# Spreading the stores of turned outputs over several steps, and one more step inside the block inverse, in a hybrid mLSTM / gated DeltaNet layer on one Trainium2 core

## The chip, the cores and the metric

The kernel runs on one core of a Trainium2 chip. The core has a matrix engine (TensorE, PE in the profile), a vector engine (VectorE, DVE), a scalar engine (ScalarE, ACT), a general one (GpSimd, POOL) and a synchronization engine (SyncE, SP) that here does nothing but issue transfers. ACT issues transfers too, from the same queue from which it computes. The metric is the device time of one execution in microseconds; lower is better. A time is given as the median of several runs.

## The reference

One layer on x of 512 tokens by 2048, all in float32. The input is normalised and multiplied by one combined weight matrix `w_in`; the parts of the product feed two mixers of tokens. The mLSTM has 8 heads (query and key 128 wide, value 256), the gated DeltaNet 16 heads of 128. Their gated, normalised outputs are multiplied by the two halves of `w_out`, merged with gates, added to x and normalised. What matters here is the DeltaNet's solve with a unit lower triangular matrix in each chunk:

```python
kk = jnp.einsum('cbhtd,cbhsd->cbhts', kc, kc)
a_mat = jnp.where(strict, bc[..., :, None] * kk * decay_mat, 0.0)
lhs = a_mat + jnp.eye(CHUNK, dtype=a_mat.dtype)
sol = lax.linalg.triangular_solve(lhs, rhs, left_side=True, lower=True, unit_diagonal=True)
...
y_a = jnp.matmul(h_a, w_out[:ML_WIDTH])
y_b = jnp.matmul(h_b, w_out[ML_WIDTH:])
return jax.nn.sigmoid(gate_a) * y_a + jax.nn.sigmoid(gate_b) * y_b
```

## The kernel before

The large projections make three matmuls for each weight tile: weights and inputs are each split into a high and a low part (`uh`, `ul` for the input; `wh` for a weight, cast by ACT in L135; `wl`, the remainder, by DVE in L138), and high by high, low by high and high by low are added up in PSUM (L261 to L263). The first half of the program makes the projections that need no mixing. Then come eight units of mixing, about 1060 to 1960 us; the output projection is the rest.

A unit projects K, V and Q of two DeltaNet heads, and in most units the query and key of one mLSTM head (`proj_cm`, called again and again). Behind every six matmuls of a projection stands a call of `tick()`: that is what is called a step here. Small pieces of mixing work are Python generators that `start` puts on a list; a tick resumes each one that is due, and `yield n` says in how many steps it wants to be resumed. So the order of PE's instructions is written by hand, as the generators yield. The order of the other engines is made by a scheduler from priorities and dependences: `urgent` raises a priority, and `behind("A")` places an instruction behind the newest cast of a weight on ACT (L135).

`dn_back` makes the inverse of the triangular matrix of a chunk by blocks, for both heads of the unit at once. Its first product p1 is negated by ACT (s1), its second p2 is copied by ACT and DVE into `tb` and `ta` (L955, L951), its third p3 (L959) is negated by ACT into s3 (L962), and its fourth p4 (L966) reads s3 and is copied into `tb` (L968). Two steps later `dn_chain` starts for the first head and three steps later for the second: the recurrence over the four chunks (matmuls L990 to L1009, ACT's copy w L1001).

`ml_head` mixes one mLSTM head. Its values v are loaded by L1107 into the one buffer `v1`. At its end two halves of the output, 128 columns each, are multiplied by their gates (L1155) and given to `turn`.

`turn` transposes blocks of 32x32 on DVE into a buffer `to` (L796; there are two) and starts `travel`, which finishes the transposition through DRAM: four transfers of 64 KB (L806), one for each 32 partitions. For K and Q these go out on SP, to `td`, and are read back (L811). For a turned output (`out` is true) they go out on ACT, behind the newest cast, to `hm_d` for the mLSTM and `h_d` for the DeltaNet, 3 or 5 steps after the transposition.

Transfers of SP and ACT share eight counters in turn (in the program's order they are called DMAHW0 to DMAHW7). An instruction that issues a transfer waits in its engine's queue until the one before on its counter has landed, where nothing else has told it so already; what is behind it on that engine waits as well.

Other names in the prediction: `yp` (L770) is ACT's copy of a finished projection out of PSUM, which frees the PSUM buffer for PE; `wr` is a weight tile on its way in (L174); `gb`, `nrb`, `iwb` are loads of one row for all partitions; `gz` (L1016) is a load of a DeltaNet head's gate.

Of the kernel before, what the change touches and what calls it, by code (L numbers as in the profile page):

```python
# [17 lines left out]
NC = S // P  # L18
# [24 lines left out]
BS = 32  # L43
# [12 lines left out]
def hybrid_body(  # L56
# [16 lines left out]
    nc = tc.nc  # L73
    ctx.enter_context(tc.manual_schedule(engines={mybir.EngineType.PE}))
    V, A, G, T = nc.vector, nc.scalar, nc.gpsimd, nc.tensor
# [64 lines left out]
    def behind(eng):  # L140

        return tc.issue_after(newest[eng])
# [66 lines left out]
    def urgent(level=1):  # L209
        return tc.high_priority(offset=level * PRIO)  # L210
# [6 lines left out]
    def start(gen, wait=0, by=None):  # L217
        active.append([gen, clock["t"] + wait, held["by"] if by is None else by])
# [557 lines left out]
    def silu_end(dst, then=None):  # L776
        th = wkb.tile([P, S], F32, tag="th", name="th", bufs=2)
        with behind("A"):
            A.activation(th, dst, AF.Tanh)
        V.scalar_tensor_tensor(out=dst, in0=th, scalar=1.0, in1=dst, op0=ALU.add, op1=ALU.mult)  # L780
        if then is not None:
            turn(*then)
        yield 1
# [8 lines left out]
    def turn(src, dst, out=False, lag=5):  # L792


        o = dst if dst is not src and len(dst.shape) == 3 else wk.tile([P, NC, P], F32, tag="to", name="to", bufs=2)
        V.transpose(o if len(src.shape) == 3 else o.rearrange("p n c -> p (n c)"), src)  # L796
        start(travel(o, dst, out), lag if out else 2)

    def travel(o, dst, out):

        d = dst if len(dst.shape) == 4 else dr.tile([16, BS, 4, BS], F32, tag="td", name="td", bufs=8)
        ov = o.rearrange("p n (j c) -> p (n j) c", c=BS)
        q = nc.scalar if out else nc.sync
        with behind("A") if out else urgent(2):
            for a in range(4):
                q.dma_start(d[:, :, a, :].rearrange("m r c -> r m c"), ov[a * BS:(a + 1) * BS])  # L806
        if d is dst:
            return
        yield 4
        with behind("A") if out else urgent(2):  # L810
            q.dma_start(dst, d.rearrange("(n j) r a c -> (j r) n (a c)", n=NC))  # L811
        yield 1

    def dn_front_k(hs, kq, u):
# [108 lines left out]
    def dn_back(hs, kq, u):  # L923
# [36 lines left out]
        s3 = wk.tile([P, 2 * NC, 64], F32, tag="s3", name="s3", bufs=1)  # L960
        with urgent():
            A.mul(s3[64:128], p3[64:128], -1.0)  # L962
        yield 2
        p4 = psw.tile([P, 2 * NC, 64], F32, tag="wk", name="p4")
        for g, a in G2:
            T.matmul(p4[0:64, g, :], s3[64:128, g, :], tb[64:128, g, 64:128], start=True, stop=True)  # L966
# [9 lines left out]
    def dn_chain(j, hs, kq, u):  # L976
# [54 lines left out]
        with urgent():  # L1031
            V.tensor_tensor(out=g, in0=po, in1=g, op=ALU.mult)
        turn(g, h_d[h], True, 5 if h < 2 * UNITS[-1][0] else 3)

    def dn_unit(p, mh):
# [13 lines left out]
        if mh is not None:  # L1049
            ps = proj_cm(mh, kind="m")  # L1050
            mkq = wkb.tile([P, 2, S], F32, tag="mkq", name="mkq", bufs=1)
            with urgent():
                A.mul(mkq[:, 1, :], ps[0], float(P) ** -0.5)
            with urgent():
                A.copy(mkq[:, 0, :], ps[1])
            start(ml_head(mh, mkq), 1, "B")
# [10 lines left out]
        for j in range(2):  # L1067
# [3 lines left out]
            start(silu_end(kq[j][:, 1, :], (kq[j][:, 1, :], qn)), 4 + 3 * j, front)  # L1071
        start(dn_front_q(hs, kq, u), QWAIT + 3 * last, by)
        start(dn_back(hs, kq, u), (25 if mh is None else 9) + 4 * last, by)

    def ml_head(h, kq):
        kT, qT = kq[:, 0, :], kq[:, 1, :]
        kw = wkb.tile([P, NC, P], F32, tag="mkw", name="kw", bufs=1)
        with behind("V"):
            turn(kT, kw)
# [73 lines left out]
        for i in range(2):  # L1153
            with behind("V"):
                V.tensor_tensor(out=g[i], in0=v1[:, :, i * P:(i + 1) * P], in1=g[i], op=ALU.mult)  # L1155
            turn(g[i], hm_d[2 * h + i], True)
            yield 1

    def ml_first(h):

        kq = wkb.tile([P, 2, S], F32, tag="mkq", name="mkq", bufs=1)
        for i in range(2):
            nc.sync.dma_start(kq[:, 1 - i, :], qk_d[2 * QKFIRST * i + h])
        yield 4
        yield from ml_head(h, kq)
# [481 lines left out]
```

## Time and profile before

| | |
|---|---|
| median of 3 runs | 2236.08 us (2230.81 to 2239.41) |
| the profiled execution | 2233.9 us |
| its span (first to last instruction) | 2232.1 us |
| PE busy | 2159.3 us, 97% of the span |
| DVE busy | 1671.0 us, 75% |
| ACT busy | 995.0 us, 45% |
| POOL busy | 276.6 us, 12% |
| mean transfer rate | 195 GB/s |

Rows of the timeline give the start, the duration, the engine (with a q: its queue of transfers), the line, the operation, output and inputs, how many were grouped, and in brackets how long the engine stood idle before, and what ended that. Rows of waits give who waited for whom, the time in total, how often, and the longest. Rows of windows give a stretch, its length, the busy time (and number of instructions) of PE, PEld (the loading of weights into PE), DVE, ACT and POOL, then the granted clock of PE, the DMA share and GB/s. Where an engine that waits isn't PE, the time costs nothing by itself.

### The profile page before, as it was taken

The numbers are of one execution on the slowest core, as the hardware profiler recorded it, in microseconds if no ns is written. First come the engines' busy times: TensorE is split into PE (matmuls) and PEld (weight loads), VectorE is DVE, ScalarE is ACT, GpSimd is POOL, SyncE is SP. The second block draws the span as 40 slices with busy tenths as digits, with TensorE's granted clock in tenths as the row PEclk, the third lists the DMA queues.
The fourth block names the chain that finished last, engine by engine and source line by source line (L and its number), as shares of the span: only waits on it lengthen the run. The fifth ranks groups of instructions, "written<-read, shape, count | busy, mean of one in ns | idle before, by whom it ended". The sixth has DMA issues, their size and how long they took to land. (4 is left out here: it accounts for less than half of the span.)

```text
span 2232.1 us, 31548 instructions
## 1 busy us (share of the span) xinstructions
PE 2159.3 (97%) x10592; PEld 1771.9 (79%) x10592; DVE 1671.0 (75%) x2907; ACT 995.0 (45%) x1890; POOL 276.6 (12%) x356
## 2 busy tenths in 40 slices
PE   7999999999999999999999999999999999999997
PEld 5877878888788788788878887878888887877775
DVE  5787788888878777877588876757675868667875
ACT  5444444444444343444544544444444445344344
POOL 0320000000000000000222422222222211110101
PEclk9999999999999999999999999999999999999999
DMA  5456666667667766776776767676756568695896
GB/s 156 125 174 193 199 201 201 205 202 231 197 208 228 235 210 205 229 244 192 195 189 168 179 145 174 147 172 166 178 139 167 141 153 230 186 278 184 250 317 215
DMA packets 534821, 435.81 MB, mean 195 GB/s; under 512 B 241921, under 2 KB 393698, under 8 KB 534530
## 3 DMA queue, kind: packets, MB, share of 16 engines
q1 hardware_dynamic: 425058, 357.68, 56.4%
q10 hardware_dynamic: 105568, 68.77, 9.8%
q0 software_dynamic: 4032, 7.34, 2.2%
q8 instruction: 83, 1.36, 0.3%
q14 instruction: 80, 0.66, 0.1%
HBM read 342.37 MB, written 95.49 MB: 196 GB/s over the span
## 5 line engine op out<-in xcount | busy, mean ns | idle before, releaser
L135 ACT CAST wh<-wr 128x512 fp32r<-128x512 f32 (+1 forms) x538 | 379.9, 707 | 470.9 <-PE pj L262 261.8
L138 DVE TENSOR_TENSOR wl<-wr,wh 128x512 fp32r<-128x512 f32 (+1 forms) x538 | 447.2, 834 | 178.2 <-ACT wh L135 160.2
L261 PE MATMUL pj<-uh,wh 128*128 128x512 f32 x1024 | 431.6, 421 | 4.2 <-ACT yp L770 4.2
L263 PE MATMUL pj<-uh,wl 128*128 128x512 f32 x1024 | 404.3, 395 | 0.0
L262 PE MATMUL pj<-ul,wh 128*128 128x512 f32 x1024 | 403.2, 394 | 0.0
L576 PE MATMUL ps<-wl,uh 128*128 128x512 f32 x704 | 277.3, 394 | 7.2 <-DVE wl L138 7.0
L575 PE MATMUL ps<-wh,uh 128*128 128x512 f32 x704 | 276.3, 392 | 7.0 <-DVE X L617 6.5
L577 PE MATMUL ps<-wh,ul 128*128 128x512 f32 x704 | 275.0, 391 | 0.0
L135 ACT CAST wh<-ts 128x512 fp32r<-128x512 f32 x224 | 138.2, 617 | 256.3 <-DVE ts L535 192.2
L135 ACT CAST wh<-t 128x1024 fp32r<-128x1024 f32 x112 | 117.9, 1053 | 250.9 <-PE ps L577 122.8
L263 PEld LDWEIGHTS pj<-uh,wl 128*128 128x128 f32 x1024 | 194.1, 190 | 43.3
L261 PEld LDWEIGHTS pj<-uh,wh 128*128 128x128 f32 x1024 | 195.2, 191 | 40.8 <-ACT yp L770 5.4
L576 PE MATMUL ps<-wl,suh 128*128 128x512 f32 x576 | 224.2, 389 | 1.6 <-DVE wl L138 1.6
L575 PE MATMUL ps<-wh,suh 128*128 128x512 f32 x576 | 224.5, 390 | 0.8 <-ACT qk L353 0.3
L577 PE MATMUL ps<-wh,sul 128*128 128x512 f32 x576 | 224.1, 389 | 0.0
L262 PEld LDWEIGHTS pj<-ul,wh 128*128 128x128 f32 x1024 | 195.6, 191 | 33.4
L138 DVE TENSOR_TENSOR wl<-ts,wh 128x512 fp32r<-128x512 f32 x224 | 153.6, 689 | 38.0 <-ACT wh L135 38.0
L138 DVE TENSOR_TENSOR wl<-t,wh 128x1024 fp32r<-128x1024 f32 x112 | 137.6, 1229 | 48.0 <-ACT wh L135 47.4
L576 PEld LDWEIGHTS ps<-wl,uh 128*128 128x128 f32 x704 | 132.6, 188 | 43.1 <-DVE wl L138 16.7
L575 PEld LDWEIGHTS ps<-wh,uh 128*128 128x128 f32 x704 | 132.5, 188 | 40.5 <-DVE X L617 12.7
L577 PEld LDWEIGHTS ps<-wh,ul 128*128 128x128 f32 x704 | 132.5, 188 | 26.7
L535 DVE TENSOR_TENSOR ts<-wr 128x512 f32<-128x512 f32 x112 | 77.2, 690 | 99.8 <-DMA wr<-t_d 76.0
(302 smaller groups left out, 3462.5 us busy)
## 6 DMA issues: line engine op xcount, KB each, us to landing
wr<-in_w_in_dram SPq DMA_DIRECT2D x704, 256.0 KB, 3.7
wr<-in_w_out_dram SPq DMA_DIRECT2D x138, 256.0 KB, 4.8
t_d<-ts ACTq DMA_DIRECT2D x96, 256.0 KB, 4.4
wr<-t_d SPq DMA_DIRECT2D x96, 256.0 KB, 4.1
wr<-in_w_in_dram SPq DMA_DIRECT2D x64, 128.0 KB, 3.2
xt<-in_x_dram SPq DMA_DIRECT2D x8, 512.0 KB, 7.2
tg_d<-X ACTq DMA_DIRECT2D x16, 256.0 KB, 6.1
tg_d<-to ACTq DMA_DIRECT2D x16, 256.0 KB, 5.1
```

The lines of the kernel that those rows point to most:

```text
L135: newest["A"] = A.copy(hi, src).ins
L138: newest["V"] = V.tensor_tensor(out=lo, in0=src, in1=hi.bitcast(F32), op=ALU.subtract).ins
L261: T.matmul(ps[j], hi[:, k, wsl], uh[:, kt, :], start=(kt == 0), stop=False)
L262: T.matmul(ps[j], hi[:, k, wsl], ul[:, kt, :], start=False, stop=False)
L263: T.matmul(ps[j], lo[:, k, wsl], uh[:, kt, :], start=False, stop=(kt == KT - 1))
L535: V.tensor_tensor(out=ts[:, 0, :], in0=r[:, 0, :], in1=r[:, 2, :], op=ALU.subtract)
L575: T.matmul(ps[t], ah, hi, start=(g == "A" and i == 0), stop=False, skip_group_check=True)
L576: T.matmul(ps[t], ah, lo, start=False, stop=False, skip_group_check=True)
L577: T.matmul(ps[t], al, hi, start=False, stop=(i == KH - 1), skip_group_check=True)
```

## The change

Three edits. In `travel`, a turned output's four transfers are no longer issued at one tick: each is issued by itself, behind the cast that is newest then, and the next follows one step later. The last unit's heads, with a lag of 3 steps, still issue all four at once. In `ml_head` the second half of the output is multiplied and turned four steps after the first and not one. In `dn_back` the fourth product comes three steps after the third and not two. The transfers of K and Q are written a second time and do what they did. No instruction is added or removed. Line numbers behind `travel` grow by four, so that s3 becomes L966 and the fourth product L970.

```diff
-        start(travel(o, dst, out), lag if out else 2)
-
-    def travel(o, dst, out):
+        start(travel(o, dst, out, lag > 3), lag if out else 2)
+
+    def travel(o, dst, out, apart):
 
         d = dst if len(dst.shape) == 4 else dr.tile([16, BS, 4, BS], F32, tag="td", name="td", bufs=8)
         ov = o.rearrange("p n (j c) -> p (n j) c", c=BS)
-        q = nc.scalar if out else nc.sync
-        with behind("A") if out else urgent(2):
+        if out:
             for a in range(4):
-                q.dma_start(d[:, :, a, :].rearrange("m r c -> r m c"), ov[a * BS:(a + 1) * BS])
-        if d is dst:
+                with behind("A"):
+                    nc.scalar.dma_start(d[:, :, a, :].rearrange("m r c -> r m c"), ov[a * BS:(a + 1) * BS])
+                if apart:
+                    yield 1
             return
+        with urgent(2):
+            for a in range(4):
+                nc.sync.dma_start(d[:, :, a, :].rearrange("m r c -> r m c"), ov[a * BS:(a + 1) * BS])
         yield 4
-        with behind("A") if out else urgent(2):
-            q.dma_start(dst, d.rearrange("(n j) r a c -> (j r) n (a c)", n=NC))
+        with urgent(2):
+            nc.sync.dma_start(dst, d.rearrange("(n j) r a c -> (j r) n (a c)", n=NC))
         yield 1
...
         with urgent():
             A.mul(s3[64:128], p3[64:128], -1.0)
-        yield 2
+        yield 3
         p4 = psw.tile([P, 2 * NC, 64], F32, tag="wk", name="p4")
...
             turn(g[i], hm_d[2 * h + i], True)
-            yield 1
+            yield 4
```

How this moves instructions is seen in the program's order. On ACT around s3 of unit 4, before (`hm_d<-to` is one piece of a turned output, with the counter or engine that it waits for in brackets; `wh<-wr` is the cast of a weight):

```order
L806 DMA hm_d_68<-to_14633 32x16x32 [waits DMAHW6_49,DVE_49]
L806 DMA hm_d_68<-to_14633 32x16x32 [waits DMAHW0_49]
L806 DMA hm_d_68<-to_14633 32x16x32 [waits DMAHW2_49]
L806 DMA hm_d_68<-to_14633 32x16x32 [waits DMAHW4_49]
L955 COPY tb_9101<-p2_14727 32x8x32 [waits DVE_49]
L955 COPY tb_9101<-p2_14727 32x8x32
L135 CAST wh_14768<-wr_14714 128x512 [waits DMAHW5_49,PE_49,Activation_49]
L806 DMA hm_d_68<-to_14647 32x16x32 [waits DMAHW7_49]
L806 DMA hm_d_68<-to_14647 32x16x32 [waits DMAHW2_49]
L806 DMA hm_d_68<-to_14647 32x16x32 [waits DMAHW4_49]
L135 CAST wh_14803<-wr_14765 128x512 [waits DMAHW3_49,PE_49,Activation_49]
L806 DMA hm_d_68<-to_14647 32x16x32 [waits DMAHW6_49]
```

and s3 follows. With the change:

```order
L806 DMA hm_d_68<-to_14633 32x16x32 [waits DMAHW6_49,DVE_49]
L959 COPY tb_9101<-p2_14727 32x8x32 [waits DVE_49]
L959 COPY tb_9101<-p2_14727 32x8x32
L135 CAST wh_14765<-wr_14711 128x512 [waits DMAHW5_49,PE_49,Activation_49]
L806 DMA hm_d_68<-to_14633 32x16x32 [waits DMAHW6_49]
L806 DMA hm_d_68<-to_14633 32x16x32 [waits DMAHW7_49]
L135 CAST wh_14798<-wr_14762 128x512 [waits DMAHW3_49,DMAHW4_49,PE_49,Activation_49]
L806 DMA hm_d_68<-to_14633 32x16x32 [waits DMAHW3_49]
L806 DMA hm_d_68<-to_14725 32x16x32 [waits DMAHW4_49]
L966 ACTIVATE s3_14792<-p3_14783 64x512 [waits PE_49,Activation_49]
```

Five pieces stand ahead of s3 where eight stood, and three of the second half's four come behind it. The last one ahead of it waits for counter 4.

On SP, the loads of the same place, before, with v ahead of the list:

```order
L1107 DMA v1_15434<-v_d_70 128x4x256 [waits DVE_49]
L1016 DMA gz_15068<-gz_d_72 128x4x128 [waits DVE_49]
L806 DMA td_14695<-qn_14540 32x16x32 [waits DVE_49]
L806 DMA td_14695<-qn_14540 32x16x32
L806 DMA td_14695<-qn_14540 32x16x32 [waits DMAHW3_49]
L806 DMA td_14695<-qn_14540 32x16x32 [waits DMAHW4_49]
L174 DMA wr_14800<-in_w_in_dram 128x2x128 [waits DMAHW5_49,DVE_49]
L174 DMA wr_14800<-in_w_in_dram 128x2x128 [waits DMAHW7_49]
L760 DMA gb_14861<-rows_d_66 128x512 [waits DMAHW1_49,Pool_49]
L174 DMA wr_14846<-in_w_in_dram 128x2x128 [waits DMAHW3_49,DVE_49]
L811 DMA qn_14540<-td_14695 128x4x128 [waits DMAHW5_49,DMAHW4_49,DMAHW2_49]
L174 DMA wr_14846<-in_w_in_dram 128x2x128 [waits DMAHW6_49]
```

and with the change, from the weight load on:

```order
L174 DMA wr_14795<-in_w_in_dram 128x2x128 [waits DMAHW4_49,DVE_49]
L174 DMA wr_14795<-in_w_in_dram 128x2x128 [waits DMAHW5_49]
L760 DMA gb_14859<-rows_d_66 128x512 [waits DMAHW7_49,Pool_49]
L815 DMA qn_14540<-td_14692 128x4x128 [waits DMAHW2_49,DMAHW3_49,DMAHW1_49,DMAHW0_49]
L174 DMA wr_14831<-in_w_in_dram 128x2x128 [waits DVE_49]
L174 DMA wr_14831<-in_w_in_dram 128x2x128
L760 DMA nrb_15205<-rows_d_66 128x512 [waits Pool_49]
L1111 DMA v1_15434<-v_d_70 128x4x256 [waits DMAHW4_49,DVE_49]
```

The load of v, which waits for DVE's second product of the mLSTM head, has moved behind both weight loads; it is on counter 4, on which ACT's last piece ahead of s3 then waits.

On ACT at the first mLSTM output, around the copy yp at 1138 us, before:

```order
L135 CAST wh<-wr 128x512 x4
L806 DMA hm_d<-to 32x16x32 x3
L770 COPY yp_9097<-pj 128x512
L806 DMA hm_d<-to 32x16x32
L135 CAST wh<-wr 128x512
```

and with the change:

```order
L135 CAST wh<-wr 128x512 x4
L806 DMA hm_d<-to 32x16x32
L770 COPY yp_9097<-pj 128x512
L771 ACTIVATE kq_9106<-yp_9097,convc 128x512
L135 CAST wh<-wr 128x512
L806 DMA hm_d<-to 32x16x32
```

One piece stands ahead of the copy where three stood.

On PE, two times six matmuls of a projection stood between the third product and the fourth, and now three times six; the fourth product and all that starts behind it in a unit come six matmuls later. Everything else on PE that the change does not name keeps its place.

## The prediction

> **What bounds the kernel now.** First comes the page's first part: TensorE (PE) is busy for nearly the whole span, so only the time in which it stands, or runs below its full clock, can be won.
>
> ```profile
> PE 2159.3 (97%) x10592; PEld 1771.9 (79%) x10592; DVE 1671.0 (75%) x2907; ACT 995.0 (45%) x1890; POOL 276.6 (12%) x356
> ```
>
> The change touches only the stage in which the heads are mixed, from about 1060 to 1960 us. The view of waits, cut to that window and to PE, tells what PE stood for there (us in total, times, longest):
>
> ```profile
> PE p L966 <- ACT s L962: 7.8, 4, 2.6
> PE pj L261 <- ACT yp L770: 4.2, 3, 2.1
> PE pr L990 <- DVE st L1009: 2.4, 1, 2.4
> PE py L1306 <- ACT yp L770: 2.3, 2, 1.7
> PE pw L998 <- DVE tb L968: 1.4, 1, 1.4
> ```
>
> The sum of these five rows is 18.1 us, 0.8% of the span. The largest is the very pair that the change spreads: the fourth product of the block inverse (L966) waits for ACT's negation s3 (L962) of the third product. The timeline of PE has the four places, in units 3 to 6 of the eight; the number in brackets is how long PE stood:
>
> ```profile
> 1466.07 1.14 PE L966 MATMUL p<-tb,s 64*64 64x64 f32 x16 [2.59 <-ACT s L962]
> ...
> 1578.01 1.14 PE L966 MATMUL p<-tb,s 64*64 64x64 f32 x16 [1.67 <-ACT s L962]
> ...
> 1687.88 1.14 PE L966 MATMUL p<-tb,s 64*64 64x64 f32 x16 [1.25 <-ACT s L962]
> ...
> 1800.39 1.14 PE L966 MATMUL p<-tb,s 64*64 64x64 f32 x16 [2.25 <-ACT s L962]
> ```
>
> A stop costs more than its own length where PE's clock falls behind it. The windows view of the 3.4 us behind five of these stops and one other shows it (the row at 1139.9 follows the 2.07 us wait for yp, 1389.1 the 2.4 us wait of L990, the rest follow the four rows above; the last three columns are granted clock, DMA share and GB/s):
>
> ```profile
> 1139.90:1143.30 3.40, 3.40 (x10) 2.62 (x9) 2.92 (x7) 3.26 (x7) 0.00 (x0) 0.51 1.08 164
> 1389.10:1392.50 3.40, 3.40 (x12) 2.82 (x11) 3.12 (x15) 0.00 (x0) 0.00 (x0) 0.50 0.42 98
> 1467.60:1471.00 3.40, 3.40 (x10) 2.65 (x9) 3.37 (x6) 1.50 (x3) 0.00 (x0) 0.50 0.74 199
> 1578.10:1581.50 3.40, 3.40 (x27) 2.91 (x28) 2.92 (x5) 2.91 (x5) 0.64 (x1) 1.00 0.92 239
> 1689.50:1692.90 3.40, 3.40 (x9) 2.63 (x8) 3.37 (x5) 1.40 (x3) 0.77 (x1) 0.50 0.77 195
> 1802.10:1805.50 3.40, 3.40 (x10) 2.65 (x9) 3.37 (x6) 1.32 (x3) 0.00 (x0) 0.50 0.45 133
> ```
>
> All stops of 2.07 us and more are followed by 3.4 us at half clock, which lose 1.7 us each; of the two shorter ones, 1.25 us is and 1.67 us isn't. The Trainium skill ("TensorE: Matmul & The Clock Gate", section "HAM oscillation — how this bites in real kernels") gives as the rule to leave no idle gap on PE of over some 3.4 us. By it none of these stops would slow the clock, and the sum below would lose its three 1.7 us terms (-6.0 becomes -4.3); the trace disagrees with it from 1.25 us on.
>
> Why s3 is late is read from ACT's own timeline, here of unit 4:
>
> ```profile
> 1566.91 4.62 ACTq L806 DMA_DIRECT2D hm_d<-to  x4
> 1571.57 0.74 ACT L955 COPY tb<-p 32x256 f32<-32x256 f32 x2 [5.99 <-DMA hm_d<-to]
> ...
> 1572.42 3.82 ACTq L806 DMA_DIRECT2D hm_d<-to  x3
> 1576.36 0.62 ACT L135 CAST wh<-wr 128x512 fp32r<-128x512 f32 x1 [3.41 <-PE pj L263]
> 1576.95 0.31 ACTq L806 DMA_DIRECT2D hm_d<-to  x1
> 1577.36 0.59 ACT L962 ACTIVATE s<-p 64x512 f32<-64x512 f32 x1 [0.39 <-ACT wh L135]
> ```
>
> Eight pieces of turned outputs of the mLSTM head are issued between 1566.9 and 1577.3. One issue takes 0.31 us; four take 4.62, since a piece waits on ACT's queue until an earlier transfer on its counter has landed, and everything behind it on ACT waits too. In three units what held s3 was in the end a weight load, seen through the last piece:
>
> ```profile
>   DMA wr<-in_w_in_dram: 3.2, 3
> ```
>
> (That row is from the view of L962: ACT's idle time ahead of s3, with its releaser.)
>
> **The change part by part.**
>
> *Three steps in place of two.* A step is six matmuls of 128x512:
>
> ```profile
> 1574.12 0.39 PE L261 MATMUL pj<-uh,wh 128*128 128x512 f32 x1
> ...
> 1575.49 0.39 PE L261 MATMUL pj<-uh,wh 128*128 128x512 f32 x1
> ```
>
> So 1.37 us. If s3 stayed where it is, the stops of 2.59, 1.67, 1.25 and 2.25 would be 1.22, 0.30, 0 and 0.88: -5.4 us, and at most three half clocks (-5.1). But s3 does not stay. The work on PE is the same, and everything behind the fourth product in the unit, the two chains with their copies and the gz load, starts one step later; the last unit's chains end one step nearer to the output stage, where PE does its other matmuls in the same order. I cost that at nothing: the cover is that stage's first blocks, and without it one step, 1.37 us, would be lost.
>
> *Pieces one a step, second product three steps later.* Ahead of s3 there are now five pieces, not eight. What counts is which transfer the fifth waits for. Before, the eighth piece shares its counter (6) with a weight load that was issued at 1571.97; now the fifth shares its own (4) with the 512 KB load of v, which waits for the mLSTM head's second product and goes out behind both weight loads. The order shows this in units 4 and 5. SP's timeline of before says when it gets that far:
>
> ```profile
> 1562.18 0.52 SPq L1107 DMA_DIRECT2D v<-v_d  x1
> ...
> 1571.97 0.52 SPq L174 DMA_DIRECT2D wr<-in_w_in_dram  x1
> ...
> 1575.68 1.25 SPq L174 DMA_DIRECT2D wr<-in_w_in_dram  x2
> ```
>
> and the landings of the v loads (L1107) and of the gz loads (L1016; the same view of each) take, least, median and most:
>
> ```profile
> DMA to landing us min/median/max: 3.5/5.6/6.5
> ...
> DMA to landing us min/median/max: 3.3/4.1/7.1
> ```
>
> Unit 4: the v load is issued between 1572.0, where SP got to that place, and 1575.7, behind a load on its counter. It lands 5.6 later, at 1577.6 to 1581.3. From the last piece to the fourth product it was 1578.01 - 1576.95 = 1.06, so that starts at 1578.7 to 1582.4. PE is there at 1578.01 - 1.67 + 1.37 = 1577.7. The stop is 1.0 to 4.7; I take 2.3, below the middle, since v and one gz load no longer stand ahead of the weight loads. That is over 2.07, so half clock: +0.6 + 1.7 = **+2.3** (-0.7 to +4.7).
>
> Unit 5 has the same order, and rows of its own:
>
> ```profile
> 1680.78 0.37 SPq L174 DMA_DIRECT2D wr<-in_w_in_dram  x1
> ...
> 1683.60 0.50 SPq L174 DMA_DIRECT2D wr<-in_w_in_dram  x1
> ...
> 1685.33 2.27 SPq L174 DMA_DIRECT2D wr<-in_w_in_dram  x3
> ```
>
> PE is there, by the same working, at 1688.0. With v issued between 1681.2 (right behind the first of these three, without the gap of 2.4 us that SP had here) and 1685.3 the product starts at 1687.9 to 1692.0: a stop of 0 to 4.0, taken as 2.0, its half clock as before: **+0.8** (-3.0 to +2.7).
>
> Unit 3: the fifth piece waits for a gz load, which waits for another gz load on the same counter. SP's timeline has there
>
> ```profile
> 1457.13 1.02 SPq L174 DMA_DIRECT2D wr<-in_w_in_dram  x2
> ...
> 1460.91 0.64 SPq L1016 DMA_DIRECT2D gz<-gz_d  x1
> ```
>
> The first of the two goes out between these, at 1457.1 to 1460.9; two landings of 4.1 later it is 1465.3 to 1469.1, the product starts at 1466.4 to 1470.2, PE is there at 1464.9: a stop of 1.5 to 5.3. I take 3.4: **+0.8** (-2.8, with its half clock gone, to +2.7).
>
> Unit 6 has no v load ahead of s3, but a load of a finished head that is issued ahead of SP's work on q. Here ACT's last cast and s3 went back to back:
>
> ```profile
> 1799.10 0.62 ACT L135 CAST wh<-wr 128x512 fp32r<-128x512 f32 x1 [4.37 <-DMA hm_d<-to]
> 1799.74 0.59 ACT L962 ACTIVATE s<-p 64x512 f32<-64x512 f32 x1
> ```
>
> Three pieces fewer should let that end at 1799.9 in place of 1800.3, with PE there at 1799.5: 0.4 left of 2.25, and no half clock: **-3.6** (-4.0 to -0.8). The four units together: **+0.3** (-10.5 to +9.3).
>
> *The heads' outputs ahead of yp.* ACT's and PE's timelines at the largest of the five waits for yp:
>
> ```profile
> 1132.32 5.60 ACTq L806 DMA_DIRECT2D hm_d<-to  x3
> 1137.96 0.59 ACT L770 COPY yp<-pj 128x512 f32<-128x512 f32 x1 [5.08 <-DMA v<-v_d]
> ...
> 1138.60 0.50 PE L261 MATMUL pj<-uh,wh 128*128 128x512 f32 x1 [2.07 <-ACT yp L770]
> ```
>
> Only one piece, with a counter whose earlier load is long done, now precedes that copy: 2.07 and its half clock go, **-3.8** (to 0 if that piece is caught as well). The other four yp waits, 4.2 + 2.3 - 2.07 = 4.4 us, have four pieces ahead of the copy where there were about five. One issue less is 0.31 a place, and one landing less up to the whole; I take **-2.0** (-4.4 to 0).
>
> *The rest.* The 1.4 us of L998, a DVE copy behind the fourth product, moves along with it: **-0.5** (-1.4 to 0). The 2.4 us of L990 is DVE at the other solve: **0** (-4.1 with its half clock, to +1.4 if a step later hits worse).
>
> **Sum**: +0.3 - 3.8 - 2.0 - 0.5 + 0 = **-6.0 us**; by the bounds -24.2 to +10.7. The profiled execution took 2233.9 (span 2232.1 and 1.8 around it), which gives 2227.9; it stands 2.2 below the median of 2236.1, by which it is **2230**.
>
> **The rivals.**
>
> *Full relief.* The stops at L966, L770 (both rows) and L998 vanish, 7.8 + 4.2 + 2.3 + 1.4 = 15.7, and four half clocks, 6.8: -22.5, 2213.6. For it: 5 pieces rather than 8, a step more, and loads that are issued earlier without v ahead. Against it: landing, not issuing, holds the queue (3 issues took 5.60). At least half of it comes in with a chance of 0.25.
>
> *Slower.* In units 3 to 5, s3 waits for the loads that have become later, at their late ends. The price is +2.7 + 4.7 + 2.7, and with landings of 6.5 and 7.1 in place of the medians another 0.9 + 0.9 + 3.0: +14.9, while the relief at unit 6 and yp is lost to pieces that now stand among the yp copies: 2251. It decides from v landing after some 1580 in unit 4. For it: the DMA share of 0.7 to 1.1 in the windows above, a load of 512 KB. Against it: SP has less to do ahead. Chance 0.13.
>
> *It doesn't do as it says.* Pieces go as one group or two where ACT stands behind the newest cast, and the order has them in pairs; s3 slides by the step that was granted, and the stops stay: 2236. Chance 0.17.
>
> **How the numbers follow.** The forecast has 0.45, full relief 0.25, no change 0.17, slower 0.13. By 0.5% of 2236, 11.2 us, the measurement can tell a difference. Faster by more needs most of full relief (0.23) or the low edge of the forecast (0.03): 0.26. Slower by more is most of its case: 0.10. The rest, 0.64, is within. The forecast's own range is 2221 to 2238; the range for eight in ten reaches into full relief and to the bound of +10.7: 2215 to 2243.
>
> **What would show it.** PE's waits: L970 (as L966 is then called) for s3 at 3.4, 2.3, 2.0 and 0.4 in units 3 to 6, with ACT idle ahead of s3 until a v or gz load lands; no 2.07 us stop for yp near 1136. I am wrong if s3 is no longer waited for at all (then 2214), if units 3 to 5 stop for over 4 us each, or if PE stops at a new line, such as L998, behind the later product.

## The result and the profile after

| | median of the runs | ratio to before, 95% interval | profiled execution's span |
|---|---|---|---|
| before | 2234.9 us (12 runs, 2224.6 to 2239.4) | | 2232.1 us |
| changed | 2227.8 us (12 runs, 2223.6 to 2232.6) | 0.9970 (0.9958 to 0.9982) | 2225.4 us |

The change is faster by 0.3%, about 7 us, clear of the noise and under the half per cent that one could tell without an interval. The forecast was -6.0 us. Where it comes from agrees with the forecast in part only, and in the experiments below two of the three edits, each alone, brought nothing that their intervals show.

The view of waits of the changed kernel, cut to PE and to the mixing stage (us in total, times, longest; lines are four higher than before, so L970 is the fourth product, L966 is s3, L1002 the chain's first solve, L1310 a matmul of the output projection):

```profile
PE p L970 <- ACT s L966: 4.9, 2, 2.6
PE py L1310 <- ACT yp L770: 3.5, 2, 3.2
PE pnum L1123 <- DVE c L1133: 2.6, 1, 2.6
PE pw L1002 <- DVE tb L972: 2.2, 3, 1.7
PE pr L994 <- DVE st L1013: 0.5, 1, 0.5
```

The sum is 13.7 us, where it was 18.9 with two rows of 0.4 that the prediction does not show. The stops for s3 are down from four to two, the one of 2.07 us for yp near 1136 is gone, the one of 2.42 us of the recurrence is down to 0.5, and there is a new one of 2.6 us in the mLSTM (L1123). The windows view shows the clock behind places that answer to those of before: 1131 is where yp was waited for, 1450 and 1786 are behind s3 of units 3 and 6, 1565.4 and the two rows from 1677.2 on behind s3 of units 4 and 5:

```profile
1131.00:1134.40 3.40, 3.40 (x17) 2.81 (x16) 3.30 (x9) 1.51 (x4) 0.10 (x1) 1.00 1.22 293
1450.00:1453.40 3.40, 3.40 (x27) 2.69 (x26) 1.16 (x2) 3.06 (x6) 0.00 (x0) 1.00 1.03 251
1565.40:1567.80 2.40, 2.40 (x7) 1.88 (x7) 2.40 (x4) 1.61 (x3) 0.00 (x0) 0.50 1.03 237
1677.20:1680.60 3.40, 3.25 (x19) 2.94 (x20) 1.91 (x4) 3.12 (x6) 0.00 (x0) 0.50 1.00 235
1680.60:1684.00 3.40, 3.40 (x9) 2.63 (x8) 3.37 (x7) 2.12 (x9) 0.00 (x0) 0.50 0.55 117
1786.00:1789.40 3.40, 3.40 (x21) 2.62 (x20) 1.33 (x3) 2.93 (x5) 0.00 (x0) 1.00 1.04 265
```

Two of five places are still at half clock, and these are the two units in which the order put the load of v ahead of s3. In unit 5 the half clock now lasts 6.8 us, twice as long as before. (A third stretch at half clock, of 3.4 us, is new: it follows the stop of 3.2 us for yp, at 1847.9.) In unit 4, PE's, ACT's and SP's timelines have

```profile
1563.99 1.52 PE L970 MATMUL p<-tb,s 64*64 64x64 f32 x16 [2.25 <-ACT s L966]
```

```profile
1556.93 0.62 ACT L135 CAST wh<-wr 128x512 fp32r<-128x512 f32 x1 [2.82 <-DMA hm_d<-to]
1561.34 1.91 ACTq L806 DMA_DIRECT2D hm_d<-to  x2
1563.34 0.59 ACT L966 ACTIVATE s<-p 64x512 f32<-64x512 f32 x1 [5.79 <-DMA hm_d<-to]
```

```profile
1555.78 0.47 SPq L760 DMA_DIRECT2D nrb<-rows_d  x1
1556.34 0.38 SPq L1111 DMA_DIRECT2D v<-v_d  x1
```

The fourth store, on the counter of nrb, could go at 1561.34, 5.6 us after that load was issued, and the fifth, on the counter of v, at 1562.86, 6.5 us after v was: the trace has the landing of v at 1562.84. Then s3 followed in 0.1 us. The cast ahead was done at 1557.55, and the third product at 1557.4: ACT stood for 5.79 us for stores alone.

### The profile page after: what moved, and what is told of

Its sections match the earlier page's. It is cut to its first block, busy times and chain, and to the rows that moved or that the text cites. A ratio compares the mean times of both kernels' runs of the same rounds, so it can differ in the third digit from the quotient of the medians.

```text
span 2225.4 us, 31556 instructions
## 1 busy us (share of the span) xinstructions
PE 2160.7 (97%) x10592; PEld 1773.5 (80%) x10592; DVE 1673.0 (75%) x2907; ACT 994.4 (45%) x1890; POOL 271.9 (12%) x356
## 4 chain that ended last, share of the span: by engine, by line
PE 67%; DMA 14%; DVE 9%; issue 6%; SPq 3%; ACT 2%; POOL 1%; ACTq 0%; DVEq 0%; POOLq 0%
PE ps L576 10%; PE ps L575 10%; PE ps L577 10%; PE pj L261 9%; PE pj L262 8%; PE pj L263 8%; DVE wl L138 3%; DMA wr<-t_d 3%; DMA wr<-in_w_in_dram 2%; PE py L1310 2%; PE py L1312 2%; PE py L1311 2%; DMA wr<-in_w_out_dram 1%; SPq L505 1%; ACT wh L135 1%
## 5 line engine op out<-in xcount | busy, mean ns | idle before, releaser
L261 PE MATMUL pj<-uh,wh 128*128 128x512 f32 x1024 | 428.4, 418 | 0.0
L261 PEld LDWEIGHTS pj<-uh,wh 128*128 128x128 f32 x1024 | 194.0, 189 | 35.1
```

Of the source, the lines that this page charges most:

```text
L261: T.matmul(ps[j], hi[:, k, wsl], uh[:, kt, :], start=(kt == 0), stop=False)
```

## The experiments

Each kernel is compared with the kernel before on the same chip; differences between two experiments are taken from their ratios. Beside the medians stand two numbers from each profiled execution, for the mixing stage alone: the time in which PE stood (the sum of all its gaps there), and the count of matmuls of 128x512 that took 0.63 us in place of 0.39, which is how half clock looks in the timeline. Such a matmul costs some 0.2 us more from start to start.

| kernel | median us | ratio (95%) | PE stood, us | half clock matmuls |
|---|---|---|---|---|
| before | 2235 | | 19.0 | 32 |
| step only | 2235.1 | 1.0004 (0.9990 to 1.0019) | 19.2 | 33 |
| stores spread only | 2232.6 | 0.9992 (0.9976 to 1.0007) | 18.7 | 37 |
| later turn only | 2220.1 | 0.9940 (0.9918 to 0.9963) | 11.0 | 7 |
| spread and step | 2236.2 | 0.9993 (0.9981 to 1.0004) | 17.4 | 29 |
| spread and turn | 2229.3 | 0.9974 (0.9962 to 0.9986) | 15.8 | 24 |
| turn and step | 2225.8 | 0.9956 (0.9943 to 0.9970) | 13.6 | 14 |
| all three (the change) | 2227.8 | 0.9970 (0.9958 to 0.9982) | 13.6 | 18 |
| turn only, v loaded early | 2229.2 | 0.9966 (0.9953 to 0.9979) | 15.2 | 7 |
| the change, s3 on DVE | 2226.5 | 0.9965 (0.9946 to 0.9984) | 13.3 | 17 |
| step only, tb on ACT | 2224.2 | 0.9950 (0.9933 to 0.9966) | 11.5 | 18 |
| turn and step, tb on ACT | 2217.4 | 0.9927 (0.9909 to 0.9945) | 11.5 | 15 |
| before, stores on GpSimd | 2217.4 | 0.9923 (0.9903 to 0.9942) | 9.5 | 12 |
| turn only, six steps | 2214.9 | 0.9907 (0.9888 to 0.9925) | 5.1 | 0 |

The last two columns follow the medians in the main: the mixing stage took 886.3 us before, 877.3 with the change and 863.2 with six steps, and in each of these three, less the time stood and 0.2 for each half clock matmul, some 860 are left (860.9, 860.1 and 858.1). The rest of the program varies by a few us from one profiled execution to the next with the same instructions, and a profile is one execution: that of the spread stores, for one, is the slowest of its twelve runs.

### Each edit alone

The step alone:

```diff
             A.mul(s3[64:128], p3[64:128], -1.0)
-        yield 2
+        yield 3
```

> Only the third edit: three steps between the third and fourth product, the outputs turned and stored as before. Theory (queue): what the change wins are PE's stops for ACT's copies s3 and yp and the half clocks behind them, and s3 is set by the transfer on whose counter the last piece ahead of it waits. Here eight pieces still stand ahead of s3, and in units 4 and 5 the last waits for the second half of a weight load as before, so one step more takes most of the stops of 1.67 and 1.25 (under 0.5 left each) and 1.37 of the 2.25 in unit 6; unit 3 now waits for a gz load and keeps 1 to 2.6. The 2.07 us stop for yp near 1136 stays, with its half clock. Together 5 to 8 us faster than before, 2227 to 2230. Rival (slack): the extra step is the whole change and the other two edits do nothing: 2228, as the change itself, and no stop at the fourth product in any unit. Rival (queue follows): s3 slides with the step, the stops stay: 2235.

It was no faster at all, 1.0004. Its waits in the mixing stage:

```profile
PE pw L998 <- DVE tb L968: 7.9, 6, 2.3
...
PE p L966 <- ACT s L962: 1.8, 2, 1.3
```

The stops for s3 did shrink, from 7.8 to 1.8. But 6.5 us came back at L998, the chain's first solve, which waits for DVE's copy of the fourth product. DVE's timeline in unit 4, with the step alone, and then before:

```profile
1571.80 0.75 DVE L773 SCALAR_TENSOR_TENSOR kq<-yp,convc,kq 128x512 f32<-128x512 f32 x1 [1.93 <-ACT kq L771]
...
1574.28 1.41 DVE L773 SCALAR_TENSOR_TENSOR kq<-yp,convc,kq 128x512 f32<-128x512 f32 x2
1575.72 0.68 DVE L968 COPY tb<-p 64x512 f32<-64x512 f32 x1
```

```profile
1579.35 0.99 DVE L773 SCALAR_TENSOR_TENSOR kq<-yp,convc,kq 128x512 f32<-128x512 f32 x1 [0.45 <-ACT kq L771]
...
1580.97 0.68 DVE L968 COPY tb<-p 64x512 f32<-64x512 f32 x1
```

One step later the fourth product falls among the multiply-adds of the next convolution, and DVE's order has the copy behind all it could do by then: with the step alone three multiply-adds stand ahead of it, before it was one. So the step hands the wait on from s3 to tb, with a half clock at 1577.6, 1690.2 and 1802.9 in place of 1467.6, 1689.5 and 1802.1. The expectation's three outcomes all had the loss or gain at s3, and none this place; the time is that of the third, 2235, but not for its reason, since the stops for s3 did not stay.

The spread stores alone:

```diff
-        with behind("A") if out else urgent(2):
-            for a in range(4):
-                q.dma_start(...)
+        if out:
+            for a in range(4):
+                with behind("A"):
+                    nc.scalar.dma_start(...)
+                if apart:
+                    yield 1
```

> Only the first edit: the four stores of a turned output one a step, everything else as before. Theory (queue): the 2.07 us stop for yp near 1136 goes with its half clock (-3.8) and some of the other yp stops (-1); in units 4 and 5 six pieces stand ahead of s3 and the last waits for a gz load that is issued behind the weight loads, with the fourth product due a step earlier than in the change: stops of 2 to 4 with half clocks, +2 to +6. Net between -3 and +2: 2232 to 2237. Rival (slack): nothing but the step counts, 2235 with the stops of before at the same places.

As expected: the stop near 1136 is gone and the stops for s3 are longer, 10.3 us in place of 7.8, all four followed by half clock.

```profile
PE p L970 <- ACT s L966: 10.3, 4, 3.2
```

In unit 4 six stores stand ahead of s3 where eight stood, but four of them are held for 5.83 us behind the copies of tb, where three took 3.82 before, and a last one until a gz load had landed:

```profile
1562.42 5.83 ACTq L806 DMA_DIRECT2D hm_d<-to  x4
...
1569.80 0.31 ACTq L806 DMA_DIRECT2D hm_d<-to  x1
1570.21 0.59 ACT L966 ACTIVATE s<-p 64x512 f32<-64x512 f32 x1 [1.17 <-DMA gz<-gz_d]
```

Spreading them moved three stores of the first half behind the copies of tb, nearer to s3.

The later turn alone:

```diff
             turn(g[i], hm_d[2 * h + i], True)
-            yield 1
+            yield 4
```

> Only the second edit: the second half of an mLSTM head's output is multiplied and turned four steps after the first, its four stores still at once. Theory (queue): six pieces stand ahead of s3, the last waiting for the second half of a weight load as before; stops at the fourth product within 1 us of before in units 3 to 6, three pieces still ahead of yp near 1136, so 2.07 stays. -3 to +1: 2232 to 2236. Rival (late v): the load of v, which goes out later, delays PE at another place, the products that read v: slower by 3 or more.

This is where the gain is: 0.9940, 13 us, more than the whole change, where the theory had at most 3. Both outcomes that had been written down are refuted. The waits are shorter at s3 and yp, L990 is gone from the list, only the solve's are longer, and no stop is over 2 us:

```profile
PE pw L998 <- DVE tb L968: 4.0, 3, 1.8
PE p L966 <- ACT s L962: 3.0, 4, 1.1
PE py L1306 <- ACT yp L770: 2.2, 2, 1.9
PE pj L261 <- ACT yp L770: 1.9, 2, 1.6
```

In unit 4 the same four stores go ahead of the copies of tb, but then only two, which hold ACT for 1.30 us; s3 follows in 0.1:

```profile
1549.69 3.45 ACTq L806 DMA_DIRECT2D hm_d<-to  x4
1553.18 0.74 ACT L955 COPY tb<-p 32x256 f32<-32x256 f32 x2 [4.57 <-DMA hm_d<-to]
...
1557.50 1.30 ACTq L806 DMA_DIRECT2D hm_d<-to  x2
1558.91 0.59 ACT L962 ACTIVATE s<-p 64x512 f32<-64x512 f32 x1 [3.09 <-PE pj L263]
```

### Edits in pairs

Each of the next three is the change with one edit taken back.

```diff
             turn(g[i], hm_d[2 * h + i], True)
-            yield 4
+            yield 1
```

> The change without its second edit: stores one a step and three steps before the fourth product, the second half turned one step after the first. Revised theory (queue as far as the solve): behind the fourth product stands DVE's copy tb, which the chain's first solve waits for, and DVE reaches it only behind the convolution's work on kq, which waits for ACT. So a step more at s3 moves the stop to the solve and gains little, as the step alone showed (0), and the gain of the change is the later turn's. Then this kernel lies with the pieces alone, 2230 to 2235, with waits of the solve for tb of 4 us or more in total. Rival (step and pieces work together): the stops of 2.6 to 3.2 at the fourth product, which the pieces alone had, shrink by the step and nothing takes their place: 2224 to 2228, all of the change's gain.

0.9993. The rival, that step and stores gain together, falls. The revised theory's time is close (2230 to 2235 was expected, 2236.2 measured), its place isn't right: tb makes only 2.5 us of the 17.4, and the rest is yp (4.0 in two rows), kq (3.7 in two rows), s3 (3.7) and the recurrence (3.2).

```diff
             A.mul(s3[64:128], p3[64:128], -1.0)
-        yield 3
+        yield 2
```

> The change without its third edit: two steps before the fourth product. In units 4 and 5 the last piece ahead of s3 waits for the load of v, as in the change. Theory (queue): the stops of 2.25 and 2.60 grow by a step to 3.6 and 4.0, units 3 and 6 get 0.5 to 1.4: 3 to 5 us slower than the change, 2230 to 2233. Rival (turn alone carries it): the pieces do no harm beside the turn, 2220 to 2224 as with the turn alone.

2229.3, a little under the 2230 to 2233 of the theory and not the 2220 to 2224 of the rival: beside the later turn, spreading the stores costs 0.0034 of the ratio, 7.6 us. The stops for s3 are 9.2 us, up from 3.0 with the turn alone. One of them, 3.87 us, is in unit 3, for which 0.5 to 1.4 had been expected; another 3.7 us, at the recurrence, had not been expected at all.

```diff
-                with behind("A"):
-                    nc.scalar.dma_start(...)
-                if apart:
-                    yield 1
+                nc.scalar.dma_start(...)      # all four behind one cast
```

> The change without its first edit: the four stores of a half still at once, the second half turned four steps after the first, three steps before the fourth product. Theory (queue as far as the solve): the stops of about 1 us at the fourth product that the turn alone had go, and come back at the solve behind DVE's tb: 2218 to 2223, no better than the turn alone (2220) by more than 2. Rival (step is worth its 1.37 us a unit): 4 to 6 faster than the turn alone, 2214 to 2216. Rival (step does harm): over 2225, with more half clocks.

2225.8, over the 2218 to 2223 of the theory and just over the bound of the rival that the step does harm. The stops for s3 are gone; 5.6 us stand at the solve behind tb, two of them over 2 us, and 2.3 at the recurrence. By the ratios the step costs 3.6 us beside the turn, though the two intervals overlap.

### Why the later turn gains

With the turn alone two things change: fewer stores stand ahead of s3, and the load of v goes out later, since its buffer is read by the second half's product. Here both halves are multiplied at the first half's time, and only the transposition and the stores of the second come four steps later:

```diff
         for i in range(2):
             with behind("V"):
                 V.tensor_tensor(out=g[i], in0=v1[:, :, i * P:(i + 1) * P], in1=g[i], op=ALU.mult)
+        for i in range(2):
             turn(g[i], hm_d[2 * h + i], True)
-            yield 1
+            yield 4
```

> The turn alone, but both halves are multiplied at the first half's time and only the second's transposition and stores come four steps later, so that the buffer of v is free, and the 512 KB load of v goes out, as early as in the kernel before. It tells apart why the later turn gains 15 us. Theory (fewer stores in the burst): six stores ahead of s3 as with the turn alone: 2219 to 2224. Rival (late v): the gain is that the load of v no longer stands ahead of the transposition of q and the weights on SP and in the DMA engines; then with v early most of it is lost, 2229 to 2235, with stops of 1.5 us and more and half clocks at the fourth product again.

2229.2, at the edge of the rival's range. By the ratios, 0.9966 against 0.9940, 5.8 us of the 13.4 are lost, and the mixing stages differ by 5.6 (877.1 against 871.5). One stop of 2.5 us for s3 is back, without the half clocks that the rival had. What is left, 0.9966, is clear of the kernel before, so the later stores gain by themselves; that the late v adds to it rests on two intervals that overlap, on the two profiles, and on what the traces show near 1136. Three stores stand ahead of yp with v early (first two rows) as with v late (last two):

```profile
1132.81 5.46 ACTq L806 DMA_DIRECT2D hm_d<-to  x3
1138.32 0.59 ACT L770 COPY yp<-pj 128x512 f32<-128x512 f32 x1 [4.95 <-DMA hm_d<-to]
```

```profile
1128.21 2.29 ACTq L806 DMA_DIRECT2D hm_d<-to  x3
1130.54 0.59 ACT L770 COPY yp<-pj 128x512 f32<-128x512 f32 x1 [1.77 <-DVE tmp L881]
```

The same three stores take 5.46 us in the one case and 2.29 in the other. What differs is the transfer on the third store's counter. With v early it is v itself: issued at 1132.11, it lands at 1137.94, and the store goes at 1137.97. With v late (1133.80) it is a weight load, which lands at 1130.17, and the store goes at 1130.19. The traces have the same split in all eight kernels with three stores there: where the load of v is issued ahead of the third store (before, the step alone with tb on either engine, and v early) the third store goes when v lands, and the three take 5.5 to 6.6 us; in the four with the later turn and without spread stores (four steps, six steps, and turn and step with tb on either engine) they take 2.3 to 3.7. So the late load of v, which the prediction had only as a cost, is here a gain.

### Is it ACT's queue?

The changed kernel with s3 on DVE:

```diff
-            A.mul(s3[64:128], p3[64:128], -1.0)
+            V.tensor_scalar(out=s3[64:128], in0=p3[64:128], scalar1=-1.0, scalar2=None, op0=ALU.mult)
```

> The changed kernel, with the negation s3 of the third product on DVE instead of ACT, the same numbers computed. Theory (queue): the two stops left at the fourth product (2.25 and 2.60) and their half clocks (about 3.4 together) come from ACT's queue alone; DVE has no stores in its queue, so both go: 6 to 9 us faster than the change, 2219 to 2222. Rival (DVE is as late): DVE is busy for 75% of the span and would hold s3 behind a weight's remainder: stops of 1 us in more units, 2226 to 2230. Rival (the third product is late itself): the stops stay whichever engine negates.

2226.5, about 1 us faster than the change, which the intervals can't tell from nothing. The stops at the fourth product went, as the theory had it, and the time did not; it lies in the range of the first rival, but s3 has no stop of the kind that this rival had:

```profile
PE pw L1002 <- DVE tb L972: 6.3, 3, 2.3
```

The 4.9 us at s3 turned into 4.1 more at the solve, as with the step, and 1.5 more at the recurrence. A copy that comes earlier gained nothing here: the next one in the chain is DVE's and, as the step alone showed, stands behind a convolution, which itself waits for ACT's yp and kq. So the copy of the fourth product was moved, for the step alone and for turn and step:

```diff
-            V.tensor_copy(tb[0:64, :, 64:128], p4[0:64])
+            A.copy(tb[0:64, :, 64:128], p4[0:64])
```

> The step alone, with the copy of the fourth product into tb on ACT instead of DVE, the same numbers computed. With the step alone DVE made that copy behind the multiplications of v and three multiply-adds of the next convolution, and PE stood for 1.9, 2.3 and 1.9 us at the solve in units 4 to 6, each with a half clock. Theory (the step hands the stop to DVE): on ACT the copy stands behind the two yp copies and is made some 2 us earlier, so these stops and their half clocks go: 9 to 12 us faster than the step alone, 2223 to 2227. Rival (the chain is late anyway): the solve waits for something else as long, 2232 to 2236.

> The later turn and the step without the spread stores, and the copy of the fourth product into tb on ACT. Turn and step together still had 5.7 us at the solve, two of the stops over 2 with half clock. Theory (the step hands the stop to DVE): they go, and what is left in the units is yp and one wait of L990: 6 to 9 us faster than turn and step (2226), 2217 to 2220, and no slower than the turn alone. Rival (ACT is the bound with its stores): tb on ACT waits behind stores, 2224 to 2230.

2224.2 and 2217.4: both times within what the theory had written down. With the step alone, moving one copy of 0.7 us in each unit to another engine gains 12 us by the ratios, and the row of the solve behind tb, which had 7.9, is gone from its waits. With turn and step it is 2.9, behind ACT now, in place of 5.6. What is first in the list with the step alone is then yp at L261, with 4.7 us.

Then the stores were taken out of ACT's queue altogether, with everything else as before the change:

```diff
-        q = nc.scalar if out else nc.sync
+        q = nc.gpsimd if out else nc.sync
```

> The kernel before, with the stores of turned outputs issued by GpSimd instead of ACT; nothing else is moved. Theory (ACT's queue): with no stores in ACT's queue the stops for s3 and yp (7.8 + 4.2 + 2.3 in the kernel before) go to under 4 in total, unless GpSimd, 12% busy, gets late itself and with it what it computes (then PE waits for products of GpSimd or what follows them). If ACT's queue is the cause and GpSimd copes: 2215 to 2224. Rival (the data is late, not the queue): the stops for s3 stay at 6 or more; 2233 to 2238.

2217.4 (0.9923): 17 us from the one word. Not one stop for s3 is left, and of the five stops for yp two, in all 2.8 us:

```profile
PE pr L990 <- DVE st L1009: 6.7, 2, 4.9
PE py L1306 <- ACT yp L770: 2.8, 2, 2.5
```

So s3, and yp in the main, were late through the stores that ACT issued. (GpSimd's stores have counters of their own as well, so which share of it is the queue and which the shared counters is not told apart.) A new stop of 4.9 us is at the recurrence. A store costs GpSimd 0.65 us against 0.31 on ACT, but GpSimd issued none in the 17 us ahead of this stop; what PE waited for is DVE's copy st, and DVE had stood for 9.47 us for a load of the next inverse (`ls<-ld`, read by L881). Why this load came later was not tried.

Last, the turn alone with six steps between the halves in place of four:

```diff
             turn(g[i], hm_d[2 * h + i], True)
-            yield 1
+            yield 6
```

> The turn alone, with six steps between the halves of an mLSTM head's output instead of four (one before). No store stands between the copies of tb and s3 in units 3 to 6; the second half's four come behind s3. Theory (fewer stores ahead): the stops of 1.06, 0.2, 0.75 and 1.02 for s3 that the turn alone had go, the stops for yp behind them grow by one to three issues: 2215 to 2222. Rival (the stores only change places): yp waits for them as long as s3 did, with half clocks: 2225 to 2232.

2214.9 (0.9907), 21 us faster than before and 14 than the change by the ratios, and the lowest median of all, though its interval overlaps those of the two kernels at 2217.4. The load of v goes out later still, so the gain is not split here between fewer stores and a late v. Its waits:

```profile
PE py L1306 <- ACT yp L770: 2.4, 2, 1.5
PE pr L990 <- DVE st L1009: 1.7, 1, 1.7
PE pj L261 <- ACT yp L770: 1.0, 2, 0.6
```

In unit 4 the last four stores of the burst are behind s3 and yp, which start as soon as PE has made their inputs:

```profile
1551.64 3.25 ACTq L806 DMA_DIRECT2D hm_d<-to  x4
...
1558.43 0.59 ACT L962 ACTIVATE s<-p 64x512 f32<-64x512 f32 x1 [0.69 <-PE p L959]
1559.96 0.58 ACT L770 COPY yp<-pj 128x512 f32<-128x512 f32 x1 [0.94 <-PE pj L263]
...
1561.16 0.31 ACTq L806 DMA_DIRECT2D hm_d<-to  x1
```

## Why the prediction was right in sum, and where its steps were wrong

The time, -6.0 forecast and -7.1 measured, and the direction are right. By its steps:

- **Unit 4** (a stop of 2.3 with half clock, from the counter that the fifth store shares with v): 2.25, with half clock, and the fifth store released when v landed, 6.5 us after it was issued. Right in mechanism and size.
- **Unit 5** (2.0, half clock as before): 2.60, from the same counter, and 6.8 us at half clock in place of 3.4. Right in mechanism; with +0.8 summed, the unit lost 3.1 (1.35 more in the stop, 1.7 more in the clock).
- **Unit 6** (0.4 left, no half clock): no stop, no half clock. Right.
- **Unit 3** (a stop of 3.4, half clock as before): no stop. This is the step that failed most, by 5.1 us: +0.8 was summed, and 2.59 and a half clock went. The term mis-sized is the time at which the first of the two gz loads goes out. ACT's timeline shows the last store ahead of s3 gone and s3 done at 1450.84, with the third product at 1446.89 and three steps behind it: just in time.

```profile
1448.92 1.23 ACTq L806 DMA_DIRECT2D hm_d<-to  x2
1450.25 0.59 ACT L966 ACTIVATE s<-p 64x512 f32<-64x512 f32 x1 [3.96 <-PE pj L263]
```

  SP's timeline in the kernel before (first row) and with the change (the other two) has

```profile
1451.61 5.42 SPq L806 DMA_DIRECT2D td<-qn  x4
```

```profile
1435.29 2.09 SPq L812 DMA_DIRECT2D td<-qn  x4
...
1438.51 0.47 SPq L1020 DMA_DIRECT2D gz<-gz_d  x1
```

  The fifth store did wait for the second gz load: that one was issued at 1442.76 and landed at 1449.82, and the store went at 1449.84. But the prediction had put SP where the kernel before had it. Measured from the fourth product (1464.9 in the prediction, 1451.13 here), it let the first gz load go out at 1443 to 1447, and SP issued it at 1438.51. The four transfers of q ahead of it took 2.09 us of SP's time in place of 5.42; v stood ahead of them before and does not now, and that this is the cause is likely but was not tried. The earlier start made up for the landings, which took 3.1 and 7.1 us where twice 4.1 was summed.
- **yp near 1136** (-3.8, since one store precedes the copy where three did): gone, with its half clock. The reason given is one of two: the turn alone still has three stores there and no stop, since the third no longer waits for v. Both edits remove this stop, and only one removal counts.
- **The other stops for yp** (4.4 to 2.4): 3.5, nearly all in one stop of 3.2 with a new half clock behind it. The term was too good by 1.1, and by 2.8 with the half clock.
- **The solve behind tb** (L998 "moves along", -0.5): +0.8 in the change. Here the step of the working itself is wrong. A copy behind the fourth product was taken to keep its place in DVE's queue when the product moved by a step; it does not, and with the step alone 6.5 us came back there for the 6.0 that s3 had given.
- **L990** (0): 2.42 fell to 0.5, and its half clock went, 3.6 us that were held possible (-4.1 was the bound) and not taken. "DVE at the other solve" was too short a reading: the copy st that PE waited for stood on DVE behind a first step of the next inverse (L881, on its 32x32 diagonal blocks), for whose load DVE stood 6.99 us (4.91 with the change):

```profile
1386.47 0.19 DVE L881 TENSOR_TENSOR tmp<-ls,xi 128x31 f32<-128x31 f32 x1 [6.99 <-DMA ls<-ld]
```

  In all fourteen profiles DVE stands at this place, for 4.5 to 9.5 us, and PE's stop behind it goes from nothing, at 4.5, to 4.9 us, at 9.5. So the term belongs to a load, as those of s3 do. What brought the load forward was not tried.
- **L1123** (not named): a new 2.59, without half clock. It is 2 us or more in just two of the fourteen profiles, the change and the change with s3 on DVE. ACT's kq, on which DVE's work ahead of it waited, had stood for 2.08 us behind two spread stores of `h_d` in the change. By the prediction's own last sentence, a stop at a new line is a sign of being wrong, and this is one.
- **The parts.** That the sum came out right is luck, since errors of both signs met: unit 3 and L990 gave 8.7 us more than summed, and unit 5, the other stops for yp, the solve and L1123 took some 9 back. (In the mixing stage PE stood 5.3 us less and ran 3.4 us less at half clock, which makes some 7; the stage of the profiled execution is 9.0 us shorter, the median 7.1. The 2 us between are not accounted for.) The working laid the gain to the step (-5.4, less what s3 slid) and to the stores (-3.8 and -2.0), and the later turn was charged with the cost of a late v. The runs show the reverse: step 0, spread stores 0 within their intervals, later turn -13.4 by its ratio; and beside the later turn the step and the spread stores cost 3.6 and 7.6 of that, both together 6.7. (The interval of the turn alone overlaps that of turn and step, and just touches those of the other two.) What carried the argument, that s3 and yp wait on ACT behind stores which wait for other transfers, is shown by the stores on GpSimd, and for single stores by the landings in the traces.
- **The rivals.** Full relief did not come with this change, but the turn alone at six steps came near to what it described (2214.9, where it had 2213.6). "Slower" had the right place, units 4 and 5 behind v, and not the size. "It doesn't do as it says" is true of the third edit alone: the stop slides on with the step.

The Trainium skill's rule on the clock ("TensorE: Matmul & The Clock Gate", section "HAM oscillation — how this bites in real kernels"), that idle gaps over about 3.4 us are what to avoid, did not hold here either: of 36 stops between 2.07 and 4.9 us in the mixing stage of the fourteen profiles, 31 are followed by matmuls at half clock, and 27 of these 31 are under 3.4.

## What to carry to other kernels

Look at what an in-order engine issues between its own computations: a transfer that must wait for an unrelated one to land holds the next copy by microseconds, where issuing it takes 0.3. Count such transfers ahead of each copy that the busiest engine waits for, put the whole burst behind that copy or on an engine with time to spare, and only then grant slack in steps; a step granted to one copy is lost at the next one in the chain unless that moves too. Measure the edits of a bundle one by one: here one of three made all the gain, and by the medians the other two took half of it back.

## What the runs showed of the hardware that was not expected

The half clock behind a stop of PE does not go by the length of the stop alone: beside the 31 of 36 stops of 2.07 us and more, 13 of 47 stops between 1.0 and 2.05 us are followed by it, and single stops of 2.48, 2.58 and 2.59 are not. The clock's rows in the traces show more. In each of the thirteen profiles that have any in the mixing stage, the stretches at half clock there begin on one grid in time with cells of 3.413 us, and last one or two cells (in the kernel before, the second begins 73 cells behind the first). What goes with them is how long PE stood within one cell. Of the cells at full clock in which it stood for 1.95 us or more, all 30 were followed by a cell at half clock; from 1.5 to 1.95 us, 11 of 21; from 1.0 to 1.5, 1 of 24; below that, none. So a stop of one length can cost its half clock or not, as it falls. In the changed kernel, L1123's 2.59 us lay across two cells (the first two rows; the clock stayed full), and most of unit 5's 2.60 in one (the third row; the next two cells ran at half clock):

```profile
1250.50:1253.90 3.40, 2.56 (x12) 1.79 (x10) 1.76 (x4) 1.32 (x3) 2.21 (x4) 1.00 1.02 268
1253.90:1257.30 3.40, 1.66 (x7) 1.43 (x8) 3.40 (x7) 3.27 (x15) 0.03 (x1) 1.00 0.22 37
1673.80:1677.20 3.40, 0.95 (x5) 0.45 (x3) 0.00 (x0) 0.49 (x1) 0.64 (x1) 1.00 0.83 244
```

Here each 3.4 us at half clock cost 1.7 us, and the kernel with six steps, whose longest stop in the stage is 1.72, has no matmul at half clock there at all.

A store from GpSimd takes its queue 0.65 us where ACT's takes 0.31 (both as medians, `hm_d<-to`), with about the same time to landing (3.9 us in the median over all stores and td transfers of that run, 3.4 before).
